# An encoder layer of Conformer convolution and dilated attention on one core: the order of a fused pair's sums, of its background, and of the q and k groups

## The chip, the cores and the metric

The kernel runs on one core of one Trainium2 chip. The metric is the device time of one launch in microseconds (us). The core's engines each work through a queue of their own: TensorE does the matmuls (PE; its loading of the stationary operand is shown as PEld), VectorE (DVE) and ScalarE (ACT) work on tiles, GpSimd (POOL) and SyncE (SP) issue transfers here.

## What is computed

One layer with 256 positions, width 4096, 16 heads of 128, and a convolution of 31 taps over 2048 channels, all float32:

```python
xn = rms_norm(x, norm_g[l])
h = jnp.einsum('bsd,de->bse', xn, w_in[l])          # 4096 x 14336
c_val, c_glu, c_gate, q, k, v, a_gate = jnp.split(h, split_pts, axis=-1)
conv_out = conformer_conv(c_val, c_glu, ...)        # GLU, depthwise conv31, LayerNorm, silu
conv_out = conv_out * jax.nn.silu(c_gate)
q, k = rms_norm(q, q_norm_g[l]), rms_norm(k, k_norm_g[l])   # per head
attn = longnet_mixture(q, k, v, rel_bias)           # three dilated windows, combined
attn_out = attn * jax.nn.silu(a_gate)
mixed = jnp.concatenate([conv_out, attn_out], axis=-1)
x = x + jnp.einsum('bse,ed->bsd', mixed, w_out[l])  # 4096 x 4096
```

## The kernel before

**Groups, pairs and parts.** The two large products are cut into 18 groups of 1024 columns: 14 of the input product (four conv, two gate, then qk and agv by turns, four of each: agv holds the attention's gate and v) and 4 of the output. A group runs through 16 pairs of 128-row blocks of the contraction; a pair's weights, 1 MB, are one transfer into one of three buffers `raw` (`load_pair`, L226, on SP's queue). In the text a pair's place in its group is its slot, counted from 0.

Float32 is done as sums of products of split numbers: a high part (`ScalarE` casts, `wh`) and a low part (`VectorE` subtracts, `wl`). A product of a split row block with a split weight takes three matmuls of 512 columns: high by high, low by high, high by low.

- A **plain pair** (`split_plain`, L973, and `Stream.plain`, L1139) takes 24 matmuls. ACT casts `wh` in two halves (L977), DVE subtracts 2048 columns for `wl` (L984).
- A **fused pair** (`split_fused`, L990, and `fused`, L1112) does a 2 x 2 block product with seven products instead of eight (Winograd's form of Strassen's scheme): 21 matmuls. It needs sums of the weight blocks (t1, t3, t4, t2) and sums of the row blocks (`block_sums`, s1 to s4). Its weights are made in four steps. Each casts on ACT and subtracts on DVE: `b` (b11 and b21, L1001 and L1002), b22 (L1014, L1015), t13 and t42 (L1001 and L1002 again). The sums themselves are taken in place in `raw` by DVE: the pair for t13 at L1016, those for t42 at L1023 and L1024. The four products m1, m5, m6 and m7 of all fused pairs of a group gather in four PSUM banks of their own and are combined by `add_more` (L1167).

Groups 0 and 1 work on x without its RMS factor and use `split_one` and `products`; while group 1 runs, `split_xn` makes the normalised rows `nh`, `nl` that all later input groups use. Groups 2 to 7 have fused pairs at slots 2, 4, 6, 8 and 10, groups 8 to 13 none. The first output group has three (slots 12 to 14), the others seven (slots 2, 4, 6, 7, 9, 10, 12).

**What sets the order.** Each engine's queue is written in program order, as the code runs: the code is a planner in Python. `Stream.step` issues the next step of weight splitting as soon as its buffers are free (four tiles `ws` of 2048 columns, and up to four `c4` tiles near fused pairs), and PE's matmuls free them. Between matmuls, `pump` gives turns to generators (the lanes): convolution, transposes through DRAM, head norms, softmax, and so on. This is the background. It goes by two budgets `left` for DVE and ACT, filled by `credit` with a share FILL of the time that PE takes, and spent by the costs that the generators yield; `now` is the planner's clock. `fused` calls `pump` twice within a fused pair.

The convolution's taps are done in two ways: on DVE alone (L524, four instructions a tap), or as products on ACT (L484, four instructions into the one tile `cp`) that DVE adds in one instruction (L515). The first way is used only in groups without fused pairs.

Heads need a PSUM bank from the tag `side`; fused pairs hold all of these, so the first fused pair of the first output group stands behind the last head (`busy`).

Of the kernel before, what the change touches and what calls it, by code (L numbers as in the profile page):

```python
# [17 lines left out]
P = 128  # L18
S = 256
# [16 lines left out]
FILL, SAVED = (0.96, 0.93), (700, 700)  # L36
# [3 lines left out]
C4 = 17  # L40
# [52 lines left out]
ONE, TWO = ((1, 0),), ((0, 2), (1, 0))  # L93
# [31 lines left out]
def layer_kernel(  # L125
# [35 lines left out]
    def rsqrt(src, shape, mul, eps, name):  # L161
# [8 lines left out]
        yield cost  # L170
        nc.scalar.activation(r, v, AF.Sqrt)
        yield
# [32 lines left out]

    def credit(ns):

        for i in range(2):
            left[i] += FILL[i] * ns
        now[0] += ns  # L210
# [19 lines left out]
    xh, xl, xsum = {}, {}, {}  # L230
# [40 lines left out]
    def split_xn(k):  # L271
# [10 lines left out]
        xh[k], xl[k] = h, l  # L282
        yield 415
        if k % 2 and k // 2 in FUSED[FUSED_IN[0]]:
            sums = block_sums(k // 2, src_of=xT, parts=(xh, xl), out=xsum, name="xs")
            if k < KT // 2:
                yield from sums
            else:
                late_sums.append(sums)

    split_gens, late_sums = [], deque()

    def run(gen):
        for cost in gen:
            spend(*(cost if isinstance(cost, tuple) else (cost or 0,)))

    def split_more():

        for gen in list(split_gens):
            cost = next(gen, None)  # L300
            if cost is None:
                split_gens.remove(gen)
            else:
                spend(*(cost if isinstance(cost, tuple) else (cost,)))

    def block_sums(j, src_of, parts, out, name):
# [14 lines left out]
        nc.scalar.copy(both[:, 0], t)  # L321
        nc.vector.tensor_sub(both[:, 1], t, both[:, 0].bitcast(F32))
# [7 lines left out]
        yield 690, 620  # L330
# [5 lines left out]
    def finish_rstd():  # L336
        tot = const.tile([P, 2], F32, name="sstot")
        nc.vector.reduce_sum(tot, ss, axis=AX.X)
        r = yield from rsqrt(tot, [P, 2], 1.0 / D, NORM_EPS, "rx")
# [127 lines left out]
    cp = const.tile([P, 4, S], F32, name="cp")  # L467


    taps, made = deque(), []  # L470
# [4 lines left out]
    def conv_products(cb):  # L475
# [4 lines left out]
        while taps and taps[-1][0] == cb:  # L480
            _, k = taps.pop()
            sh, lo, hi = conv_range(k)
            for t in range(4):
# [4 lines left out]
                if t == 3:  # L488
                    made.append((k, now[0] + 1500))
                if t % 2:  # L490
                    yield 0, 1020
            while made:
                yield

    def conv_gen(cb):
# [15 lines left out]
        while n_left:  # L511
            if made and made[0][1] <= now[0]:
                k, _ = made[0]
                _, lo, hi = conv_range(k)
                nc.vector.tensor_add(c[:, :, lo:hi], c[:, :, lo:hi], cp[:, :, lo:hi])  # L515
# [16 lines left out]
            if n_left == 6 and cb < 3 and cb + 1 not in fetched:  # L532
                fetched.add(cb + 1)
                post_lane.add(fetch_gen(cb + 1))
# [31 lines left out]
    def ln_gen():  # L566
# [5 lines left out]
        yield  # L572
# [3 lines left out]

        sq = [t4(f"sq{cb}") for cb in range(4)]
        for cb in range(4):
            nc.scalar.activation(sq[cb], cT[cb], AF.Square)
            yield 0, 1050  # L580
        pv = yield from channel_mean(sq, "va", sq[0])
        r = yield from rsqrt(pv[:, :S], [P, S], 1.0, LN_EPS, "rc")
        for cb in range(4):
            nc.vector.tensor_mul(cT[cb], cT[cb], bcast4(r))
            yield 1220
        for cb in range(4):
# [44 lines left out]
    def qk_norm(hg):  # L631
        st = sb.tile([P, 16], F32, tag="rs_small", bufs=6, name=f"ssqk{hg}")
        both = (qt[hg], kt[hg])
        for i, src in enumerate(both):
            v = src.rearrange("p a b -> p (a b)")
            for n in range(8):
# [5 lines left out]
                if n % 4 == 3:  # L642
                    yield 0, 1960
        r = yield from rsqrt(st, [P, 16], 1.0 / DH, NORM_EPS, f"rqk{hg}")
        for i, src in enumerate(both):
            v = src.rearrange("p a b -> p (a b)")
            for n in range(8):
# [4 lines left out]
                if n % 4 == 3:  # L652
                    yield 0, 1600
        yield from turn_far([qt[hg], kt[hg]], f"turn_qk{hg}")
# [4 lines left out]
    def head_gen(hg, hh):  # L659
# [32 lines left out]
        yield 1370  # L692
        for it in range(2):
# [4 lines left out]
        yield 0, 1380  # L698
        nc.vector.reciprocal(z, z)
        yield 160  # L700
        for it in range(2):
# [3 lines left out]
        yield 0, 1000  # L705
        tmp = t2(f"turn_p{h}")
# [54 lines left out]
    post_lane, head_lane, gate_lane, mix_lane = Lane(2), Lane(4), Lane(1, ()), Lane(1)  # L761
# [570 lines left out]
```

## Time and profile before

| what | us |
|---|---|
| three runs: lowest, median, highest | 1691.78, 1695.71, 1695.84 |
| the profiled execution | 1695.4 |
| its span, from the first to the last instruction | 1693.6 |
| mean granted TensorE clock | 0.990 |

A line of the timeline gives start, length, engine, source line, operation, the tile written and the tiles read (without their numbers), and in brackets how long the engine had been idle before and what it waited for. A line of the waits gives who waited for whom, with the time in all, how often, and the longest. A line of the busy time by stretch gives the stretch, its length, then for each engine its busy time and number of instructions, the granted clock, the share of the transfers and their GB/s. A line of the groups gives busy time and mean ns of one, then the engine's idle time just before them.

### The profile page before, as it was taken

How to read it: one execution, taken by the hardware profiler on the slowest of the kernel's cores; microseconds unless marked ns; L12 is line 12 of the kernel's file. 1: busy time of each engine (PE TensorE's matmuls, PEld its weight loads, DVE VectorE, ACT ScalarE, POOL GpSimd, SP SyncE). 2: the span in 40 equal slices, each digit the busy share in tenths (PEclk: the TensorE clock that was granted, in tenths of full speed). 3: DMA queues.
4: the chain of work that ended last, by engine and by line, in shares of the span. 5: the costliest groups of instructions: out<-in, count | busy, mean ns of one | idle time of the engine just before them, and what ended most of it. 6: DMA issues, size and time to landing. Idle time of an engine off the chain costs nothing.

```text
span 1693.6 us, 18693 instructions
## 1 busy us (share of the span) xinstructions
PE 1613.2 (95%) x6904; PEld 1296.9 (77%) x6904; DVE 1280.0 (76%) x1414; ACT 977.2 (58%) x1525; POOL 99.0 (6%) x184
## 2 busy tenths in 40 slices
PE   9999999999999989899999999999999999798988
PEld 7888768777777767678887887788888877586866
DVE  6669878787777777779788788877476677787877
ACT  6756545465646455577676657558667444444443
POOL 0000000000000000011110300102112100000000
PEclk9999999999999999999999999999999999999999
DMA  9766456454655554478675754866676745464653
GB/s 381 273 250 250 149 183 206 183 199 158 227 208 187 189 172 175 151 249 267 210 236 191 251 198 174 260 238 230 213 265 214 247 160 181 176 223 178 220 189 124
DMA packets 64523, 357.22 MB, mean 211 GB/s; under 512 B 9104, under 2 KB 11920, under 8 KB 27824
## 3 DMA queue, kind: packets, MB, share of 16 engines
q1 hardware_dynamic: 54096, 326.38, 54.4%
q0 software_dynamic: 10048, 29.37, 5.8%
q8 instruction: 54, 0.88, 0.2%
q10 hardware_dynamic: 288, 0.28, 0.1%
q14 instruction: 37, 0.30, 0.1%
HBM read 337.09 MB, written 18.91 MB: 210 GB/s over the span
## 4 chain that ended last, share of the span: by engine, by line
PE 52%; DVE 24%; ACT 14%; issue 9%; DMA 1%; ACTq 0%; DVEq 0%
PE c L1147 24%; PE c L1149 12%; ACT wh L977 7%; ACT t L1001 5%; DVE t L1002 5%; DVE b L1002 4%; PE acc L885 3%; PE acc L886 3%; PE acc L888 3%; DVE wl L984 3%; DVE raw L1016 3%; PE c L1162 2%; DVE raw L1024 2%; DVE raw L1023 2%; DVE b L1015 2%
## 5 line engine op out<-in xcount | busy, mean ns | idle before, releaser
L984 DVE TENSOR_TENSOR wl<-raw,wh 128x2048 fp32r<-128x2048 f32 x202 | 461.9, 2289 | 188.4 <-ACT wh L977 187.1
L977 ACT CAST wh<-raw 128x1024 fp32r<-128x1024 f32 x404 | 401.7, 1044 | 137.8 <-PE c L1149 95.6
L1147 PE MATMUL c<-wh,nh 128*128 128x512 f32 x1200 | 471.7, 393 | 4.0 <-ACT wh L977 3.8
L1149 PE MATMUL c<-wh,nl 128*128 128x512 f32 x1200 | 469.9, 392 | 0.0
L1001 ACT CAST t<-raw 128x1024 fp32r<-128x1024 f32 x108 | 113.2, 1048 | 336.0 <-DVE raw L1016 186.1
L1147 PE MATMUL c<-wl,nh 128*128 128x512 f32 x1200 | 299.6, 392 | 0.0
L1147 PEld LDWEIGHTS c<-wh,nh 128*128 128x128 f32 x1200 | 227.9, 190 | 54.9 <-ACT wh L977 6.5
L1149 PEld LDWEIGHTS c<-wh,nl 128*128 128x128 f32 x1200 | 227.3, 189 | 47.7
L1147 PEld LDWEIGHTS c<-wl,nh 128*128 128x128 f32 x1200 | 225.2, 188 | 47.0 <-DVE wl L984 0.3
L1002 DVE TENSOR_TENSOR t<-raw,t 128x1024 fp32r<-128x1024 f32 x108 | 132.3, 1225 | 126.0 <-ACT t L1001 126.0
L484 ACT ACTIVATE cp<-a,wT 128x241 f32<-128x241 f32 (+13 forms) x288 | 125.1, 491 | 108.7 <-DVE cT L515 108.6
L1147 PE MATMUL c<-wh,mh 128*128 128x512 f32 x288 | 113.9, 396 | 0.0
L1149 PE MATMUL c<-wh,ml 128*128 128x512 f32 x288 | 113.5, 394 | 0.0
L956 DVE TENSOR_TENSOR wh<-raw,wh 128x1024 fp32r<-128x1024 f32 x63 | 77.0, 1222 | 39.5 <-ACT wh L955 39.1
L885 PE MATMUL acc<-wh,xh 128*128 128x512 f32 x256 | 99.9, 390 | 0.5 <-ACT xh L264 0.5
L886 PE MATMUL acc<-wh,xl 128*128 128x512 f32 x256 | 99.7, 390 | 0.0
L955 ACT CAST wh<-raw 128x1024 fp32r<-128x1024 f32 x63 | 66.2, 1050 | 42.6 <-PE acc L888 26.9
L515 DVE TENSOR_TENSOR cT<-cT,cp 128x964 f32<-128x964 f32 (+13 forms) x72 | 84.6, 1175 | 2.9 <-ACT cp L484 0.8
L524 DVE SCALAR_TENSOR_TENSOR cT<-a,wT,cT 128x255 f32<-128x255 f32 (+8 forms) x192 | 80.9, 474 | 0.7
L1147 PE MATMUL c<-wl,mh 128*128 128x512 f32 x288 | 71.5, 390 | 0.0
L888 PE MATMUL acc<-wh,xh 128*128 128x512 f32 x256 | 69.1, 389 | 0.0
L1002 DVE TENSOR_TENSOR b<-raw,b 128x1024 fp32r<-128x1024 f32 x54 | 65.8, 1219 | 0.7 <-ACT b L1001 0.7
(321 smaller groups left out, 2129.9 us busy)
## 6 DMA issues: line engine op xcount, KB each, us to landing
raw<-in_w_dram SPq DMA_DIRECT2D x286, 1024.0 KB, 4.9
xT<-in_x_cols_dram SPq DMA_DIRECT2D x15, 512.0 KB, 6.8
x<-in_x_dram SPq DMA_DIRECT2D x8, 512.0 KB, 8.5
xr<-in_x_dram SPq DMA_DIRECT2D x8, 512.0 KB, 6.5
out_dram<-xr SPq DMA_DIRECT2D x15, 256.0 KB, 7.0
T<-bias_dram SPq DMA_DIRECT2D x16, 192.0 KB, 5.8
raw<-in_w_dram SPq DMA_DIRECT2D x3, 512.0 KB, 6.0
turn_qk0d<-turn_qk POOLq DMA_DIRECT2D x2, 512.0 KB, 8.6
```

The costliest lines, as they stand in the source:

```text
L484: nc.scalar.activation(cp[:, t, lo:hi], a[:, t, lo + sh : hi + sh], AF.Copy, scale=wT[:, 4 * cb + t, k : k + 1],)
L515: nc.vector.tensor_add(c[:, :, lo:hi], c[:, :, lo:hi], cp[:, :, lo:hi])
L524: nc.vector.scalar_tensor_tensor(c[:, t, lo:hi], a[:, t, lo + sh : hi + sh], wT[:, 4 * cb + t, k : k + 1], c[:, t, lo:hi], op0=ALU.mult, o ...
L885: nc.tensor.matmul(a, hs, wp, start=k == 0, stop=False)
L886: nc.tensor.matmul(a, ls, wp, start=False, stop=False)
L888: nc.tensor.matmul(a, hs, wp, start=False, stop=k == KT - 1)
L977: nc.scalar.copy(h[:, 1024 * k : 1024 * k + 1024], raw_tiles[u][:, k])
L984: nc.vector.tensor_sub(l, src, h.bitcast(F32))
L1001: nc.scalar.copy(h, src)
L1002: nc.vector.tensor_sub(l, src, h.bitcast(F32))
L1147: nc.tensor.matmul(acc, a[s][0], b[e], start=begin, stop=False)
L1149: nc.tensor.matmul(acc, a[s][1], b[e], start=False, stop=False)
```

## The change

- In `split_fused` the sum for t13 moves from the second step to the end of the first, and the sums for t42 from the third to the end of the second.
- `fused` no longer calls `pump`; while a fused pair or a row block is waited for, `more_rows` gives turns to the row splits alone. In groups with fused pairs the background's share of ACT's time (FILL) falls from 0.93 to 0.72.
- The order of groups 6 to 13 becomes qk, qk, agv, qk, agv, qk, agv, agv.
- Products of taps have two tiles `cp`, used by turns; a product is added, and its tile used again, 3 us of the planner's clock later. Taps on DVE alone may now also be issued in fused groups, with 0.4 us of budget to spare.
- Generators wait 3 us of the planner's clock (`settled`) between steps of one engine and the next engine's step on them.
- Group 1 is done by `Stream.group` with plain pairs; `split_xn` follows it pair by pair, at most four at a time, into `xnh`, `xnl`, and the sums of its rows are made right there.
- The first output group has four fused pairs (slots 8, 10, 12, 14) in another order of pairs. A plain pair's two casts are two steps. One `c4` buffer fewer (16).

```diff
-FILL, SAVED = (0.96, 0.93), (700, 700)
+FILL, SAVED = ((0.95, 0.72), (0.96, 0.93)), (700, 700)
+SETTLED = 3000
-C4 = 17
+C4 = 16
...
-for _hg in range(4):
-    GROUPS.append(("qk", _hg, C_Q + 512 * _hg, C_K + 512 * _hg))
-    GROUPS.append(("agv", _hg, C_AG + 512 * _hg, C_V + 512 * _hg))
+for _kind, _hg in zip("kkakakaa", (0, 1, 0, 2, 1, 3, 2, 3)):
...
-FUSED += [range(3)] + 3 * [range(7)]
+FUSED += [range(4)] + 3 * [range(7)]
-ORDERS += [(3, 4, 5, 8, 9, 10, 11, 12, 13, 14, 15, 6, 0, 1, 2, 7)]
+ORDERS += [(4, 5, 8, 9, 10, 11, 12, 13, 0, 14, 1, 15, 2, 6, 3, 7)]
...
+    def settled():
+        end = now[0] + SETTLED
+        while now[0] < end:
+            yield
...
-            left[i] += FILL[i] * ns
+            left[i] += FILL[state["taps"]][i] * ns
...
-            if made and made[0][1] <= now[0]:
-                k, _ = made[0]
+            if made and made[0][2] <= now[0]:
+                k, cp, _ = made.popleft()
                 nc.vector.tensor_add(c[:, :, lo:hi], c[:, :, lo:hi], cp[:, :, lo:hi])
-                made.clear()
+                cps.append((cp, now[0] + SETTLED))
...
-            elif taps and state["taps"]:
+            elif taps and left[0] > (0 if state["taps"] else 400):
...
+    def more_rows():
+        if split_gens:
+            split_more()
+        else:
+            pump(PRODUCT)
...
             def one():
-                both("b", blocks()[:, 0:2, :], ("b11", "b21"))
+                r = blocks()
+                both("b", r[:, 0:2, :], ("b11", "b21"))
+                nc.vector.tensor_add(r[:, 0:4:3, :], r[:, 0:3:2, :], twice(r[:, 3, :]))
+                spend(1225)
...
             def two():
                 nc.scalar.copy(h, r[:, 2, :])
                 nc.vector.tensor_sub(l, r[:, 2, :], h.bitcast(F32))
-                nc.vector.tensor_add(r[:, 0:4:3, :], r[:, 0:3:2, :], twice(r[:, 3, :]))
-                spend(1910, 620)
+                nc.vector.tensor_add(r[:, 2, :], r[:, 0, :], r[:, 2, :])
+                nc.vector.tensor_add(r[:, 1, :], r[:, 2, :], r[:, 1, :])
+                spend(2050, 620)
...
             def three():
                 both("t13", blocks()[:, 0:4:3, :], ("t1", "t3"))
-                r = blocks()
-                nc.vector.tensor_add(r[:, 2, :], r[:, 0, :], r[:, 2, :])
-                nc.vector.tensor_add(r[:, 1, :], r[:, 2, :], r[:, 1, :])
-                spend(1365)
...
-            return [(ONE, high), (ONE, low)]
+            return [(ONE, first), (NONE, lambda: high(1)), (ONE, low)]
...
+                if g == 1 and slot % 2 == 0 and slot < n_pairs - 2:
+                    load_xT(2 * slot + 4, 4, nc.sync)
...
                 if slot < n_pairs - 1:
                     self.plain(u, j, rows, one, slot == 0)
+                    if g == 1:
+                        split_gens.extend(split_xn(k) for k in (2 * j, 2 * j + 1))
...
-                if i in (2, 5):
-                    pump()
...
-        if g >= FUSED_IN[0]:
+        if g > 0:
             stream.group(g)
```

How the instructions move is shown at three places. In the names the first number is that of the pair, 16 to a group; `wl` is the low part of a plain pair, `b`, `b22`, `t13` and `t42` are the four splits of a fused pair, and a row that writes `raw` is a sum taken in place.

First, VectorE in group 16, the third output group, slots 3 and 4 (pairs 259 and 260). Before:

```order
L984 TENSOR_TENSOR wl259_10909<-raw259_10791,wh259_10894 128x2048
L1002 TENSOR_TENSOR b_2601_10920<-raw260_10834,b_2600_10919 128x1024
L1015 TENSOR_TENSOR b22_260_10923<-raw260_10834,b22_260_10923 128x512
L1016 TENSOR_TENSOR raw260_10834<-raw260_10834 128x2x512
L1002 TENSOR_TENSOR t13_260_10936<-raw260_10834,t13_260_10936 128x1024
L1023 TENSOR_TENSOR raw260_10834<-raw260_10834 128x512
L1024 TENSOR_TENSOR raw260_10834<-raw260_10834 128x512
L1002 TENSOR_TENSOR t42_260_10947<-raw260_10834,t42_260_10947 128x1024
```

And now:

```order
L1028 TENSOR_TENSOR wl259_10878<-raw259_10760,wh259_10863 128x2048
L1046 TENSOR_TENSOR b_2601_10889<-raw260_10803,b_2600_10888 128x1024
L1054 TENSOR_TENSOR raw260_10803<-raw260_10803 128x2x512
L1062 TENSOR_TENSOR b22_260_10893<-raw260_10803,b22_260_10893 128x512
L1063 TENSOR_TENSOR raw260_10803<-raw260_10803 128x512
L1064 TENSOR_TENSOR raw260_10803<-raw260_10803 128x512
L1046 TENSOR_TENSOR t13_260_10907<-raw260_10803,t13_260_10907 128x1024
L1046 TENSOR_TENSOR t42_260_10916<-raw260_10803,t42_260_10916 128x1024
```

The first sum moved from behind b22 to behind b, and the two small sums from behind t13 to ahead of it; t13 and t42 now follow each other.

Second, VectorE in group 2 (the first with fused pairs), the fused pair at slot 2 (pair 34), where `xs` and `xsp` are the sums of the rows for pair 8. Before:

```order
L1016 TENSOR_TENSOR raw34_1513<-raw34_1513 128x2x512
L1002 TENSOR_TENSOR t13_34_1652<-raw34_1513,t13_34_1652 128x1024
L1023 TENSOR_TENSOR raw34_1513<-raw34_1513 128x512
L1024 TENSOR_TENSOR raw34_1513<-raw34_1513 128x512
L314 TENSOR_TENSOR xs_8_1665<-xT16_1143 128x128
L315 TENSOR_TENSOR xs_8_1665<-xs_8_1665,xT16_1143 128x128
L317 TENSOR_TENSOR xs_8_1665<-xT16_1143 128x128
L318 TENSOR_TENSOR xs_8_1665<-xT16_1143,xs_8_1665 128x128
L322 TENSOR_TENSOR xsp8_1670<-xs_8_1665,xsp8_1670 128x512
L1002 TENSOR_TENSOR t42_34_1673<-raw34_1513,t42_34_1673 128x1024
```

And now:

```order
L1046 TENSOR_TENSOR b_341_1589<-raw34_1490,b_340_1588 128x1024
L1054 TENSOR_TENSOR raw34_1490<-raw34_1490 128x2x512
L1062 TENSOR_TENSOR b22_34_1593<-raw34_1490,b22_34_1593 128x512
L1063 TENSOR_TENSOR raw34_1490<-raw34_1490 128x512
L1064 TENSOR_TENSOR raw34_1490<-raw34_1490 128x512
L1046 TENSOR_TENSOR t13_34_1614<-raw34_1490,t13_34_1614 128x1024
L1046 TENSOR_TENSOR t42_34_1625<-raw34_1490,t42_34_1625 128x1024
```

The five instructions of the row sums have left the fused pair (they stand in group 1 now).

Third, ScalarE in group 4, the fused pair at slot 4 (pair 68), where `cp` is a product of a tap. Before:

```order
L1001 CAST b_680_2908<-raw68_2820 128x1024
L1014 CAST b22_68_2912<-raw68_2820 128x512
L1001 CAST t13_68_2925<-raw68_2820 128x1024
L484 ACTIVATE cp_77<-a0_1047,wT_73 128x247 x2
L1001 CAST t42_68_2938<-raw68_2820 128x1024
L484 ACTIVATE cp_77<-a0_1047,wT_73 128x247 x2
L977 CAST wh69_2961<-raw69_2862 128x1024 x2
```

And now:

```order
L1045 CAST b_680_2880<-raw68_2795 128x1024
L1061 CAST b22_68_2885<-raw68_2795 128x512
L1045 CAST t13_68_2899<-raw68_2795 128x1024
L1045 CAST t42_68_2908<-raw68_2795 128x1024
L495 ACTIVATE cp1_78<-a0_1065,wT_73 128x244 x2
L1022 CAST wh69_2931<-raw69_2837 128x1024 x2
```

No product stands between the casts of t13 and t42 any more; one pair of products is left, ahead of the next plain pair's wh.

More of the change, by code (lines that the diff above doesn't have):

```diff
@@ L170, in rsqrt @@
         yield cost
+        if wait:
+            yield from settled()
         nc.scalar.activation(r, v, AF.Sqrt)
-        yield
+        yield 0, 1400 + n
+        if wait:
+            yield from settled()
         nc.vector.reciprocal(r, r)
@@ L281, in split_xn @@
         nc.vector.tensor_sub(l, src, h.bitcast(F32))
-        xh[k], xl[k] = h, l
+        xnh[k], xnl[k] = h, l
         yield 415
         if k % 2 and k // 2 in FUSED[FUSED_IN[0]]:
[L285 to L295, printed above, removed]
+            yield from block_sums(k // 2, src_of=xT, parts=(xnh, xnl), out=xsum, name="xs")
+    split_gens = deque()
     def split_more():
-        for gen in list(split_gens):
+        for gen in list(split_gens)[:4]:
             cost = next(gen, None)
@@ L329, in block_sums @@
         out[j] = names
-        yield 690, 620
+        yield 690
     def by_block(ap):
@@ L465, in fetch_gen @@
         yield 0, 1150
-    cp = const.tile([P, 4, S], F32, name="cp")
-    taps, made = deque(), []
+    taps, made = deque(), deque()
+    cps = deque((const.tile([P, 4, S], F32, name=f"cp{i}"), 0) for i in range(2))
     def conv_range(k):
@@ L571, in ln_gen @@
         nc.scalar.copy(mu, pm[:, :S])
-        yield
+        yield 0, 400
+        yield from settled()
         for cb in range(4):
@@ L585, in ln_gen @@
             yield 1220
+        yield from settled()
         for cb in range(4):
@@ L692, in head_gen @@
         yield 1370
+        yield from settled()
         for it in range(2):
@@ L705, in head_gen @@
         yield 0, 1000
+        yield from settled()
         tmp = t2(f"turn_p{h}")
@@ L827, in evacuate_sum @@
         fused = (g, e) in more_tiles
-        if not fused and s == 0:
+        if not fused and s == 0 and (g, e) != (1, 1):
             plain_tiles[(g, e)] = half_tile(g, e)
-        tile_, pair = (more_tiles if fused else plain_tiles)[(g, e)]
+        tile_, pair = (more_tiles if fused else plain_tiles).get((g, e)) or plain_tiles[(g, 0)]
         t = pair[:, s, :]
```

109 lines of the change are left out of this document (67 added, 42 removed).

## The prediction

> **What bounds the kernel now.** I read the page first, then the busy time by stretch, then the waits, then the engines' timelines in one fused pair. The page's engine line is tempting: TensorE (PE) busy 95%, so little to win.
>
> ```profile
> span 1693.6 us, 18693 instructions
> PE 1613.2 (95%) x6904; PEld 1296.9 (77%) x6904; DVE 1280.0 (76%) x1414; ACT 977.2 (58%) x1525; POOL 99.0 (6%) x184
> ```
>
> But a matmul is drawn 0.39 us long and the next one starts before it ends, so busy time hides lost time. The pace is better read from starts. In the timeline of PE in a stretch without waits, one plain pair begins at 773.85 and the next at 779.29:
>
> ```profile
> 768.57 3.61 PE L678 MATMUL psc<-qk,near_q 128*128 128x256 f32 x16
> 771.83 2.18 PE L1147 MATMUL c<-wl,nh 128*128 128x512 f32 x8
> 773.85 0.39 PE L1147 MATMUL c<-wh,nh 128*128 128x512 f32 x1
> ...
> 779.29 0.39 PE L1147 MATMUL c<-wh,nh 128*128 128x512 f32 x1
> ```
>
> So 24 matmuls take 5.44 us, 0.2267 us each; a fused pair (21) takes 4.76 at that pace. The 16 records of four heads take 771.83 - 768.57 = 3.26 us, 0.204 each. Now the busy time by stretch, cut where groups begin (start; groups 0-1; 2-7; 8-13; output; columns are length, busy of PE, PEld, DVE, ACT and POOL with counts, PE clock, DMA):
>
> ```profile
> 0.00:5.60 5.60, 4.10 (x22) 3.91 (x22) 0.59 (x2) 2.00 (x4) 0.20 (x4) 1.00 0.61 180
> 5.60:180.40 174.80, 174.75 (x769) 144.17 (x770) 126.25 (x193) 113.33 (x184) 2.87 (x5) 1.00 0.77 286
> 180.40:747.30 566.90, 528.79 (x2217) 417.62 (x2216) 435.19 (x409) 313.25 (x459) 11.50 (x21) 0.98 0.53 188
> 747.30:1301.90 554.60, 549.17 (x2420) 453.27 (x2419) 427.09 (x518) 377.57 (x683) 74.06 (x135) 1.00 0.68 225
> 1301.90:1689.90 388.00, 356.41 (x1482) 277.90 (x1480) 290.12 (x294) 171.01 (x199) 10.39 (x19) 0.98 0.54 192
> ```
>
> Groups 2-7 need 6 x (11 x 24 + 5 x 21) = 2214 matmuls, 501.9 us: 65.0 are lost. Groups 8-13 need 2304 and some 116 records of heads and means, 522.3 + 23.7 = 546.0: 8.6 lost. Output needs 375 + 3 x 363 = 1464 and 16 records, 335.2: 52.8 lost. Groups 0-1 lose 0.7. So 127 us are lost, nearly all in the two stretches that hold fused pairs, whose clock is also 0.98 where the others show 1.00. The floor is 1693.6 - 127.1 = 1566.5. The waits name the place:
>
> ```profile
> DVE t L1002 <- ACT t L1001: 126.0, 108, 1.5
> ACT wh L977 <- PE c L1149: 95.6, 44, 6.9
> PE m L1036 <- ACT t L1001: 41.6, 44, 2.7
> PE m L1038 <- DVE t L1002: 27.6, 55, 0.5
> ```
>
> PE waits for the split of the sums (t, that is t13 and t42 of a fused pair), and in 108 splits of 108 VectorE (DVE) stands idle for ScalarE (ACT) first. One plain and one fused pair of group 16, DVE and then ACT:
>
> ```profile
> 1510.45 2.29 DVE L984 TENSOR_TENSOR wl<-raw,wh 128x2048 fp32r<-128x2048 f32 x1 [0.67 <-ACT wh L977]
> 1512.66 1.22 DVE L1002 TENSOR_TENSOR b<-raw,b 128x1024 fp32r<-128x1024 f32 x1
> 1513.79 0.69 DVE L1015 TENSOR_TENSOR b<-raw,b 128x512 fp32r<-128x512 f32 x1
> 1514.39 1.22 DVE L1016 TENSOR_TENSOR raw<-raw 128x1024 f32<-128x1024 f32 x1
> 1516.81 1.23 DVE L1002 TENSOR_TENSOR t<-raw,t 128x1024 fp32r<-128x1024 f32 x1 [1.20 <-ACT t L1001]
> 1517.95 0.69 DVE L1023 TENSOR_TENSOR raw<-raw 128x512 f32<-128x512 f32 x1
> 1518.67 0.69 DVE L1024 TENSOR_TENSOR raw<-raw 128x512 f32<-128x512 f32 x1
> 1520.56 1.23 DVE L1002 TENSOR_TENSOR t<-raw,t 128x1024 fp32r<-128x1024 f32 x1 [1.19 <-ACT t L1001]
> 1522.45 2.29 DVE L984 TENSOR_TENSOR wl<-raw,wh 128x2048 fp32r<-128x2048 f32 x1 [0.67 <-ACT wh L977]
> ```
> ```profile
> 1510.32 1.05 ACT L1001 CAST b<-raw 128x1024 fp32r<-128x1024 f32 x1
> 1511.27 0.61 ACT L1014 CAST b<-raw 128x512 fp32r<-128x512 f32 x1
> 1515.72 1.05 ACT L1001 CAST t<-raw 128x1024 fp32r<-128x1024 f32 x1 [3.84 <-DVE raw L1016]
> 1519.47 1.05 ACT L1001 CAST t<-raw 128x1024 fp32r<-128x1024 f32 x1 [2.70 <-DVE raw L1024]
> 1520.43 1.99 ACT L977 CAST wh<-raw 128x1024 fp32r<-128x1024 f32 x2
> ```
>
> The unit repeats every 12.0 us (1510.45 to 1522.45), where PE needs 45 x 0.2267 = 10.2. The two engines take turns: DVE sums, ACT casts the sum, DVE takes the difference, twice over.
>
> **The sums, moved.** Nothing is added; the order shows raw (the sum for t13) right behind b, and both later sums ahead of t13's difference. Working the after unit from the starts above: wl to b 2.21, b to raw 1.13, raw to b22 1.14 (as t13 to the next sum), b22 to the first small sum 0.60, to the second 0.72, from there to ACT's cast of t42 0.80, to wh 0.96, to the next wl 2.02: 9.58 us. The cast of t13 (1.33 behind its sum's start, 1.05 long) now lies beside b22 and the small sums; DVE's wait before t42 shrinks to about 0.1. What is late next is PE: 9.58 is under 10.2. Each unit had lost 1.8 and more, and now gains 0.6 of lead. Two fused pairs in a row (two places in groups 15-17) remain DVE's: 1.13 + 1.14 + 0.60 + 0.72 + 0.72 + 1.14 + 1.14 = 6.59 against 4.76, so 1.8 of lead is spent at each. The lead on entry comes from t42 of the first fused pair; in group 3, before, the pair's first matmul and the end of t42 are:
>
> ```profile
> 287.81 0.39 PE L1036 MATMUL m<-b,nh 128*128 128x512 f32 x1
> ...
> 289.64 1.22 DVE L1002 TENSOR_TENSOR t<-raw,t 128x1024 fp32r<-128x1024 f32 x1 [1.17 <-ACT t L1001]
> ```
>
> PE needs t42 18 matmuls after 287.81, at 291.9; it is done at 290.86, 1.0 early. With the sums moved it comes 2.4 sooner (12.0 - 9.58), 3.4 early.
>
> **Background out of fused pairs.** In group 2 the five sums of xn leave the fused pair; elsewhere a conv product or a transpose stood there, as here, ahead of a plain pair's wl:
>
> ```profile
> 571.55 1.89 DVE L417 STREAM_TRANSPOSE turn_g<-gate 128x512 f32<-128x512 f32 x3
> ```
>
> What was in the fused stretch must go into plain slots, where DVE was busy 427.09 of 554.6 us, so it is covered. What stays in the stretch (one or two conv adds a group) costs 1.2 us each at most, against the lead above. On ACT a pair of products (2 x 0.49) now stands between t42 and wh: such a unit is 9.58 + 0.98 = 10.56 by ACT, 0.36 over PE; four of them spend 1.4 of 3.4 us. If that cover fails, the next part's rival A gives the price.
>
> **Two tiles of products.** These rows price a tap:
>
> ```profile
> L484 ACT ACTIVATE cp<-a,wT 128x241 f32<-128x241 f32 (+13 forms) x288 | 125.1, 491 | 108.7 <-DVE cT L515 108.6
> L515 DVE TENSOR_TENSOR cT<-cT,cp 128x964 f32<-128x964 f32 (+13 forms) x72 | 84.6, 1175 | 2.9 <-ACT cp L484 0.8
> L524 DVE SCALAR_TENSOR_TENSOR cT<-a,wT,cT 128x255 f32<-128x255 f32 (+8 forms) x192 | 80.9, 474 | 0.7
> ```
>
> In the changed order 49 taps instead of 72 go through ACT. DVE gains 23 x (4 x 0.474 - 1.175) = 16.6 us of work, ACT loses 23 x 4 x 0.491 = 45; the second tile takes ACT's 108.6 us of waiting for DVE out of its queue. Both lie in plain slots, off PE's path: nothing, or up to 5 us if DVE falls behind there.
>
> **q and k sooner, the waits called settled, group 1 in pairs, four fused pairs in the first output group.** Settled only issues later, to work that has slack; PE still carries the same head matmuls. The last heads' po come in the fifth pair of the first output group instead of the sixth, ahead of its first fused pair (now ninth, then thirteenth); no wait is expected, 0 to 5. Group 1 lost nothing and does the same matmuls; its seven more loads of xT pass through SP's queue ahead of weights: 0 to 5. One more fused pair saves 3 matmuls, 0.7.
>
> **The clock.** A wait is followed by slow matmuls:
>
> ```profile
> 302.00:304.00 2.00, 0.90 (x3) 0.47 (x4) 1.23 (x1) 2.00 (x4) 0.00 (x0) 1.00 0.00 0
> 304.00:306.00 2.00, 2.00 (x6) 1.59 (x7) 0.78 (x1) 2.00 (x3) 0.00 (x0) 0.59 0.51 119
> 306.00:308.00 2.00, 2.00 (x6) 1.55 (x6) 2.00 (x2) 0.66 (x2) 0.00 (x0) 0.56 0.96 406
> ```
>
> By the two rows at 0.98, 0.02 x (566.9 + 388.0) = 19 of the 127 us are this. I take it to go with the waits, but 3. [...]
>
> **The sum.** Floor 1566.5 - 0.7 = 1565.8; groups 8-13 keep 8.6 (3 if the 5.4 us go in which PE was idle there, 554.60 - 549.17); groups 2-7 keep 1 each, 6 (0 to 24); output keeps 8 (2 in the first, 3 in the second, which enters behind a late fused pair, 1.5 in each other; 0 to 20); clock 3 (0 to 8). Span 1591.4. The profiled execution took 1695.4 for its span of 1693.6, 1.8 more, and stands 0.3 under the median of 1695.71: 1593.
>
> **Rivals.** A, the cover is thin: the cast chain moves from DVE's wait to ACT's queue. Units with a product and its add take 10.56 + 0.5, 0.86 over, 24 times: 21; entries find no lead, 10 groups x 1.5: 15; double fused pairs cost 1.8 x 6: 11; slots lost to clock, half of before: 10. With 8.6: 1565.8 + 8.6 + 57 = 1631, and 1633 with the 1.8. For it: 95.6 us in which wh already waited for PE's buffers, so lead cannot grow freely. Against: 3.4 us of lead on entry.
>
> B, the clock loss is not due to the waits: 1593 - 3 + 19 = 1609. Against: the two stretches at 0.98 are the two with the waits. [...]
>
> C, slower: buffers. If the cast of wh has to wait until PE has finished the fused pair before it, PE stands through both casts, 2.02 us, in each unit: 10.2 + 2.02 + 0.1 = 12.3 against 12.0, in 40 units 12 us more, 1707. It decides from 1.8 us of such wait a unit on. For it: the row of 95.6 us, 44 times, 2.2 each. Against: before, these waits lay mostly in plain stretches, and the tile's former user, the wh before it, is read out 3.6 us into a plain pair.
>
> D, the casts stay bound by something else and the unit stays 12.0: 1695. The order shows the sums moved, so little is left for it.
>
> **Chances and range.** Forecast 0.68, A 0.20, B 0.05, C 0.03, D 0.04. The likeliest gives 1593. Its own bounds are 1571 (all of it hidden: 1565.8 + 3 + 1.8) and 1628 (24, 20 and 8 with the 8.6); I take 1572, and to take in A I end at 1640. About 0.3% (5 us) is what a measurement can tell: faster by more 0.93, within 0.04, slower 0.03.
>
> **What would show it.** Right: DVE's wait for t under 30 us instead of 126; units of about 10.2 us in fused stretches; PE waits for t under 20 us in all; clock 1.00 there; groups 8-13 unchanged near 555 us. Rival A: units of 10.5 to 11 with wh or cp ending the wait. C: wh waiting for PE inside fused stretches. Wrong altogether: a span above 1640, or losses outside the fused stretches.

## The result and the profile after

| | us |
|---|---|
| changed kernel, four runs: lowest, median, highest | 1574.82, 1575.35, 1577.37 |
| kernel before, four runs beside them: lowest, median, highest | 1691.78, 1695.55, 1695.84 |
| profiled execution of the changed kernel, and its span | 1575.05, 1573.3 |

The ratio of the changed kernel to the one before is 0.9298, 95% interval 0.9282 to 0.9314: 120 us less. The forecast was 1593 in a range of 1572 to 1640, so the time lies inside, 18 under the likeliest value.

The page's engine line of the changed kernel, then its waits of PE:

```profile
span 1573.3 us, 18570 instructions
PE 1565.2 (99%) x6901; PEld 1294.9 (82%) x6901; DVE 1298.7 (83%) x1473; ACT 928.4 (59%) x1421; POOL 99.2 (6%) x184
```
```profile
PE po L740 <- DMA pr<-turn_p15d: 1.7, 1, 1.7
PE m L1082 <- DVE t L1046: 1.3, 1, 1.3
```

The two rows that carried the loss before (41.6 and 27.6 us for t) have become one wait of 1.3 us. The busy time by stretch, cut where groups begin (groups 0-1, 2-7, 8-13, output; columns as before):

```profile
5.48:181.44 175.96, 175.69 (x770) 143.86 (x769) 122.87 (x176) 107.96 (x172) 2.87 (x5) 1.00 0.77 284
181.44:683.28 501.84, 501.84 (x2216) 415.54 (x2214) 455.92 (x471) 288.83 (x395) 8.26 (x15) 1.00 0.60 212
683.28:1230.89 547.61, 547.61 (x2421) 454.45 (x2420) 421.68 (x524) 357.31 (x656) 78.05 (x142) 1.00 0.69 229
1230.89:1569.50 338.61, 335.62 (x1478) 276.77 (x1476) 296.86 (x300) 172.31 (x196) 9.79 (x18) 1.00 0.61 219
```

The clock is 1.00 in each, and in groups 2 to 13 PE is never idle in these records. Against the count of matmuls: groups 2-7 take 501.84 us where the count gives 501.9 (65.0 more before); groups 8-13 take 547.61 where it gives 546.0 (8.6 more before); the output takes 338.6 where it gives 335.2 - 0.7 = 334.5 (52.8 more before).

A plain and a fused pair of group 16 on DVE, then ACT from the same unit:

```profile
1416.35 2.29 DVE L1028 TENSOR_TENSOR wl<-raw,wh 128x2048 fp32r<-128x2048 f32 x1 [0.67 <-ACT wh L1022]
1418.55 1.22 DVE L1046 TENSOR_TENSOR b<-raw,b 128x1024 fp32r<-128x1024 f32 x1
1419.81 1.23 DVE L1054 TENSOR_TENSOR raw<-raw 128x1024 f32<-128x1024 f32 x1
1420.95 0.69 DVE L1062 TENSOR_TENSOR b<-raw,b 128x512 fp32r<-128x512 f32 x1
1421.67 0.69 DVE L1063 TENSOR_TENSOR raw<-raw 128x512 f32<-128x512 f32 x1
1422.40 0.69 DVE L1064 TENSOR_TENSOR raw<-raw 128x512 f32<-128x512 f32 x1
1423.01 2.50 DVE L1046 TENSOR_TENSOR t<-raw,t 128x1024 fp32r<-128x1024 f32 x2
1426.29 2.29 DVE L1028 TENSOR_TENSOR wl<-raw,wh 128x2048 fp32r<-128x2048 f32 x1 [0.77 <-ACT wh L1022]
```
```profile
1421.15 1.06 ACT L1045 CAST t<-raw 128x1024 fp32r<-128x1024 f32 x1 [3.37 <-DVE raw L1054]
1423.20 1.06 ACT L1045 CAST t<-raw 128x1024 fp32r<-128x1024 f32 x1 [0.99 <-DVE raw L1064]
1424.26 2.00 ACT L1022 CAST wh<-raw 128x1024 fp32r<-128x1024 f32 x2
```

ACT now casts t13 (1421.15) while DVE is at b22 and the small sums, so DVE goes from one t to the other without a break (one row, x2, 2.50 us). The unit repeats after 9.94 us instead of 12.0, under the 10.2 that PE needs. Over the whole kernel the group of these splits, 110 of them, has 2.8 us of idle time in front, against 126 before:

```profile
L1046 DVE TENSOR_TENSOR t<-raw,t 128x1024 fp32r<-128x1024 f32 x110 | 134.2, 1221 | 2.8
```

### The profile page after: what moved, and what is told of

The parts are those of the page before. It is cut to its first block, busy times and chain, and to the rows that moved or that the text cites. A ratio compares the mean times of both kernels' runs of the same rounds, so it can differ in the third digit from the quotient of the medians.

```text
span 1573.3 us, 18570 instructions
## 1 busy us (share of the span) xinstructions
PE 1565.2 (99%) x6901; PEld 1294.9 (82%) x6901; DVE 1298.7 (83%) x1473; ACT 928.4 (59%) x1421; POOL 99.2 (6%) x184
## 4 chain that ended last, share of the span: by engine, by line
PE 87%; issue 6%; DMA 4%; DVE 1%; ACT 1%; POOL 0%; SPq 0%; DVEq 0%; POOLq 0%; ACTq 0%
PE c L1195 40%; PE c L1197 20%; PE c L1210 3%; PE m L1082 3%; PE m L1080 3%; PE m L1081 3%; PE c L1080 2%; PE c L1081 2%; PE c L1082 2%; PE acc L927 2%; PE acc L924 2%; PE acc L925 2%; PE c L1212 2%; DMA raw<-in_w_dram 1%; PE psc L696 1%
## 5 line engine op out<-in xcount | busy, mean ns | idle before, releaser
L1028 DVE TENSOR_TENSOR wl<-raw,wh 128x2048 fp32r<-128x2048 f32 x217 | 496.4, 2289 | 174.3 <-ACT wh L1022 165.6
L1022 ACT CAST wh<-raw 128x1024 fp32r<-128x1024 f32 x434 | 433.6, 1048 | 255.4 <-PE c L1197 185.1
L533 DVE SCALAR_TENSOR_TENSOR cT<-a,wT,cT 128x252 f32<-128x252 f32 (+10 forms) x284 | 117.7, 472 | 0.5
L495 ACT ACTIVATE cp<-a,wT 128x241 f32<-128x241 f32 (+7 forms) x196 | 84.5, 488 | 9.9 <-DVE cT L524 9.8
L1054 DVE TENSOR_TENSOR raw<-raw 128x1024 f32<-128x1024 f32 x55 | 67.4, 1225 | 1.9
L1195 PEld LDWEIGHTS c<-wh,mh 128*128 128x128 f32 x280 | 52.6, 188 | 10.9
L1197 PEld LDWEIGHTS c<-wh,ml 128*128 128x128 f32 x280 | 52.6, 188 | 10.9
L1195 PEld LDWEIGHTS c<-wl,mh 128*128 128x128 f32 x280 | 52.6, 188 | 10.9
L998 DVE TENSOR_TENSOR wh<-raw,wh 128x1024 fp32r<-128x1024 f32 x31 | 37.9, 1224 | 24.8 <-ACT wh L997 24.8
L524 DVE TENSOR_TENSOR cT<-cT,cp 128x964 f32<-128x964 f32 (+7 forms) x49 | 57.1, 1166 | 1.1
```

Source lines behind the costliest of these rows:

```text
L495: nc.scalar.activation(cp[:, t, lo:hi], a[:, t, lo + sh : hi + sh], AF.Copy, scale=wT[:, 4 * cb + t, k : k + 1],)
L533: nc.vector.scalar_tensor_tensor(c[:, t, lo:hi], a[:, t, lo + sh : hi + sh], wT[:, 4 * cb + t, k : k + 1], c[:, t, lo:hi], op0=ALU.mult, o ...
L1022: nc.scalar.copy(h, raw_tiles[u][:, k])
L1028: nc.vector.tensor_sub(l, src, h.bitcast(F32))
L1054: nc.vector.tensor_add(r[:, 0:4:3, :], r[:, 0:3:2, :], twice(r[:, 3, :]))
L1195: nc.tensor.matmul(acc, a[s][0], b[e], start=begin, stop=False)
```

## The experiments

Times are medians. "Over the change" means against 1575.35 us of the changed kernel.

**The sums alone.** The kernel before with only the sums moved:

```diff
             def one():
-                both("b", blocks()[:, 0:2, :], ("b11", "b21"))
+                r = blocks()
+                both("b", r[:, 0:2, :], ("b11", "b21"))
+                nc.vector.tensor_add(r[:, 0:4:3, :], r[:, 0:3:2, :], twice(r[:, 3, :]))
...
             def two():
...
-                nc.vector.tensor_add(r[:, 0:4:3, :], r[:, 0:3:2, :], twice(r[:, 3, :]))
...
+                nc.vector.tensor_add(r[:, 2, :], r[:, 0, :], r[:, 2, :])
+                nc.vector.tensor_add(r[:, 1, :], r[:, 2, :], r[:, 1, :])
...
             def three():
                 both("t13", blocks()[:, 0:4:3, :], ("t1", "t3"))
-                r = blocks()
-                nc.vector.tensor_add(r[:, 2, :], r[:, 0, :], r[:, 2, :])
-                nc.vector.tensor_add(r[:, 1, :], r[:, 2, :], r[:, 1, :])
...
```

> The kernel before with the sums of a fused pair moved and nothing else. Theory S (the order of the sums is the gain: a unit of a plain and a fused pair falls from 12.0 us to 9.6, under TensorE's 10.2): 1595 to 1620 us, with VectorE's wait for t gone (under 30 us from 126). Rival P (what stood between the steps of a fused pair, the background, is the gain): 1665 to 1690. Rival O (neither alone: the new order of groups and group 1 in pairs carry it): 1650 to 1690.

Measured: 1590.13 us, ratio to before 0.9381 (0.9354 to 0.9408): 104 of the 120 us. Its longest waits of PE, and its busy time in groups 2-7 and in groups 8-13 (cut where its own groups begin):

```profile
PE c L1147 <- ACT wh L977: 3.8, 3, 1.3
PE m L1038 <- DVE t L1002: 3.7, 6, 1.2
PE m L1036 <- ACT t L1001: 2.4, 2, 1.3
```
```profile
180.34:690.16 509.82, 505.43 (x2215) 416.11 (x2214) 437.68 (x409) 314.42 (x459) 11.54 (x21) 1.00 0.58 209
690.16:1244.73 554.57, 549.34 (x2422) 453.81 (x2420) 427.51 (x518) 377.69 (x683) 74.23 (x135) 1.00 0.67 225
```

The waits for t fall from 69 to 6 us. What is left is 4.4 us of PE idle in groups 2-7 (509.82 - 505.43), all but 0.37 of it in the first 31 us of group 2, and 5.2 in groups 8-13, close to the 5.4 that the kernel before showed there. Against the changed kernel groups 2-7 take 8.0 us more (509.82 - 501.84) and groups 8-13 take 7.0 more (554.57 - 547.61). So the sums explain the fused stretches but for the head of group 2, and something else in the change took away the rest.

**The sums put back.** The changed kernel with its sums in their old places:

```diff
             def one():
...
-                nc.vector.tensor_add(r[:, 0:4:3, :], r[:, 0:3:2, :], twice(r[:, 3, :]))
...
             def two():
...
+                nc.vector.tensor_add(r[:, 0:4:3, :], r[:, 0:3:2, :], twice(r[:, 3, :]))
...
-                nc.vector.tensor_add(r[:, 2, :], r[:, 0, :], r[:, 2, :])
-                nc.vector.tensor_add(r[:, 1, :], r[:, 2, :], r[:, 1, :])
...
             def three():
                 both("t13", blocks()[:, 0:4:3, :], ("t1", "t3"))
+                r = blocks()
+                nc.vector.tensor_add(r[:, 2, :], r[:, 0, :], r[:, 2, :])
+                nc.vector.tensor_add(r[:, 1, :], r[:, 2, :], r[:, 1, :])
...
```

> The changed kernel with the sums put back to their old places. Theory S: a unit is 12.0 us again whatever else is changed, 1.8 over TensorE in 16 units of the output and 24 of groups 2 to 7 less some lead: 1650 to 1685 us, and the TensorE clock falls again to about 0.98 in these stretches. Rival P: 1575 to 1610. Rival O: 1575 to 1600.

Measured: 1677.71 us, ratio 0.9898 (0.9869 to 0.9926), 102 over the change. The waits of PE are those of the kernel before again:

```profile
PE m L1080 <- ACT t L1045: 36.5, 39, 1.3
PE m L1082 <- DVE t L1046: 22.7, 44, 0.5
```

Taken away or put in alone, the sums are worth 102 to 104 us; all the rest together is worth 15 to 17.

**Background back in fused pairs.** The changed kernel with its turns inside `fused` and the old share of ACT:

```diff
-FILL, SAVED = ((0.95, 0.72), (0.96, 0.93)), (700, 700)
+FILL, SAVED = ((0.96, 0.93), (0.96, 0.93)), (700, 700)
...
                     self.free((u, freed))
+                if i in (2, 5):
+                    pump()
```

> The changed kernel with the two turns of background inside a fused pair back, and ScalarE's share at 0.96 and 0.93 in all groups. Theory S: the unit has 0.6 us to spare and some 3 us of lead, so a little is lost in groups 2 to 7 alone: 1575 to 1595 us. Rival P: 1640 to 1690. Rival O: 1575 to 1580.

Measured: 1575.59 us, 0.2 over the change, ratio 0.9295 (0.9268 to 0.9322).

**Background out, alone.** The kernel before without the two turns:

```diff
-                if i in (2, 5):
-                    pump()
```

> The kernel before without the two turns of background inside a fused pair, and nothing else. Theory S: the unit stays 12.0 us in the output groups (no gain there) and at 12.0 to 12.5 in groups 2 to 7: 1670 to 1695 us. Rival P: 1590 to 1630. Rival O: 1685 to 1700.

Measured: 1696.71 us against 1694.4 beside it, ratio 1.0013 (1.0002 to 1.0024). Where the sums stand early, the background in fused pairs is covered; where they stand late, taking it out wins nothing, probably because DVE was waiting for ACT in any case (126.0 us for t in the kernel before). This part of the change is worth nothing in either kernel.

**One tile of products.** The changed kernel with one `cp`:

```diff
-    cps = deque((const.tile([P, 4, S], F32, name=f"cp{i}"), 0) for i in range(2))
+    cps = deque((const.tile([P, 4, S], F32, name=f"cp{i}"), 0) for i in range(1))
```

> The changed kernel with one tile for the products of taps instead of two. Theory T (in groups 8 to 13 TensorE waited because ScalarE's next product stood at the head of its queue for the one tile, with the cast of wh behind it): three to five waits of 1.3 to 1.5 us come back, 1579 to 1583 us. Rival N (the planner's settled waits took these waits away): 1574 to 1577.

Measured: 1573.51 us, ratio 0.9291 (0.9275 to 0.9308), not to be told from the change. In the profiled execution, the slowest of its four runs, PE waits for wh twice:

```profile
PE c L1195 <- ACT wh L1022: 3.3, 2, 2.8
```

One wait, 0.5 us, lies in groups 8 to 13. The long one, 2.8 us, lies before them, between 100 and 680 us (PE is busy 577.13 of these 580.00 us); what held its cast up is not shown. So one tile alone does not bring the waits of groups 8 to 13 back. But it does not bring the old way back either: with one tile that rests 3 us only 33 taps go through ACT (49 in the change, 72 before), and ACT waits 13.3 us for their adds, not 108.6.

**No settling.** The changed kernel where `settled` returns at once:

```diff
-        end = now[0] + SETTLED
-        while now[0] < end:
-            yield
+        return
+        yield
```

> The changed kernel whose generators no longer wait 3 us of the planner's clock between engines (the two tiles of products keep theirs). Theory T: 1574 to 1577 us. Rival N: waits of ScalarE and VectorE for each other at the head of their queues come back in groups 8 to 13, 1579 to 1586.

Measured: 1575.31 us, ratio 0.9291 (0.9276 to 0.9307). No difference either, and no wait of PE in groups 8 to 13. The products' own rests of 3 us are not in `settled` and stayed.

**More work per fused pair.** How much cover is left? One and two reductions more for DVE, behind the first sum of each of the 55 fused pairs; nobody reads their result:

```diff
+    idle = const.tile([P, 2], F32, name="idle")
...
                 nc.vector.tensor_add(r[:, 0:4:3, :], r[:, 0:3:2, :], twice(r[:, 3, :]))
+                for _ in range(1):
+                    nc.vector.reduce_max(idle, r[:, 1:3, :], axis=AX.X)
```

> The changed kernel with one more VectorE instruction of about 1.2 us in each fused pair, right behind the first sum (it reduces two blocks of raw to a tile that nobody reads). Theory S with its numbers (unit 9.58 us of VectorE and ScalarE against TensorE's 10.20, some 3.4 us of lead on entry to a fused stretch): the unit is 10.8, the lead covers groups 2 to 7, and the output groups with two fused pairs in a row lose about 5 us each: 1588 to 1605 us. Rival Q (VectorE has far more room than 0.6 us a unit, since steps overlap more than the starts say): 1574 to 1580.

> The same with two such instructions. Theory S: the unit is 12.0 us, as in the kernel before: groups 2 to 7 lose about 6 us each, the output groups 6 to 14 each, and the TensorE clock falls: 1650 to 1685 us. Rival Q: 1580 to 1620.

Measured: 1621.30 us with one, ratio 0.9566 (0.9547 to 0.9585), and 1691.88 with two, ratio 0.9984 (0.9973 to 0.9994). Both lie above what was expected. The waits of PE with one, and the row of the added work, then the waits with two:

```profile
PE m L1085 <- DVE t L1047: 28.7, 30, 1.6
```
```profile
L1057 DVE TENSOR_REDUCE idle<-raw 128x2 f32<-128x1024 f32 x55 | 66.6, 1211 | 0.0
```
```profile
PE m L1085 <- DVE t L1047: 61.5, 44, 1.6
PE c L1085 <- DVE b L1065: 20.1, 19, 2.2
```

The first 66.6 us of added work cost some 46, so 21 us of it were hidden; the second cost 70.6, all of it and 4 more. With one, the span is 47.4 us over the changed kernel's; of PE's 28.7 us of waits for t, 16.7 lie in groups 2-7 and 12.0 in the output. The expectation had nothing in groups 2-7: it had counted with units of 9.58 us and forgotten that many there also hold a pair of products on ACT (10.6 us, below), which have no slack to give but the lead. For the output it had about 5 us in each group with fused pairs in a row; the unit there is 9.94 and not 9.58, and fused pairs in a row cost more than was worked out (below). These reasons are argued from the rows and not tested by themselves.

**The sums of the rows back in group 2.** The changed kernel, where the sums for the row blocks of pairs 8 and 10 stand in the fused pairs of group 2 again:

```diff
-            yield from block_sums(k // 2, src_of=xT, parts=(xnh, xnl), out=xsum, name="xs")
+            sums = block_sums(k // 2, src_of=xT, parts=(xnh, xnl), out=xsum, name="xs")
+            if k < KT // 2:
+                yield from sums
+            else:
+                late_sums.append(sums)
...
+                if g == 2 and late_sums and slot % 2:
+                    run(late_sums.popleft())
```

> The kernel after, with the sums of the row blocks of pairs 8 and 10 put back into group 2's fused pairs, between t13 and t42. Theory R (these sums are the largest part of the 15 us that moving the weights' sums alone leaves over the kernel after): PE waits again for t between 190 and 215 us, 2 to 5 waits of 0.5 to 1.3 us, the clock falls there, and the time is 1578 to 1582 us. Rival (group 2 is short in the kernel after because its background is gone, wherever the row sums stand): no wait over 0.5 us there and 1574 to 1577 us.

Measured: 1578.26 us, ratio 0.9314 (0.9301 to 0.9326), 2.7 over the next experiment on the same chip (1577.08 to 1579.98 against 1575.18 to 1575.69, four runs each). DVE between t13 and t42 of the second of these pairs, then what PE waited for there:

```profile
204.99 1.22 DVE L1054 TENSOR_TENSOR t<-raw,t 128x1024 fp32r<-128x1024 f32 x1
206.12 0.28 DVE L328 TENSOR_TENSOR xs<-xT 128x128 f32<-128x128 f32 x1
...
207.82 0.69 DVE L337 TENSOR_TENSOR xsp<-xs,xsp 128x512 fp32r<-128x512 f32 x1 [0.69 <-ACT xsp L335]
208.77 1.23 DVE L1054 TENSOR_TENSOR t<-raw,t 128x1024 fp32r<-128x1024 f32 x1 [0.26 <-ACT t L1053]
```
```profile
208.79 0.50 PE L1088 MATMUL m<-t,xsp 128*128 128x512 f32 x1 [1.03 <-ACT t L1053]
210.05 0.50 PE L1090 MATMUL m<-t,xsp 128*128 128x512 f32 x1 [0.53 <-DVE t L1054]
```

Without them t42 would start at 206.12; it starts 2.65 later, and PE, not yet far behind the weights at the head of the first fused group, waits. Half of that theory holds: PE waits there again, three times, but the clock stays at 1.00 in this execution, and 2.7 us is not the largest part of 15.

**One tile, used again soon.** Does the rest of the tile keep ACT from standing in front of a product that DVE has not added yet? The changed kernel with one tile and a rest of 0.5 us instead of 3:

```diff
-    cps = deque((const.tile([P, 4, S], F32, name=f"cp{i}"), 0) for i in range(2))
+    cps = deque((const.tile([P, 4, S], F32, name=f"cp{i}"), 0) for i in range(1))
...
-                cps.append((cp, now[0] + SETTLED))
+                cps.append((cp, now[0] + 500))
```

> The kernel after, with one tile for products that may be written again 0.5 us of the planner's clock after the add that reads it, instead of two that rest 3 us. Theory H (the rest keeps ACT from standing at the head of its queue until DVE has added, and thereby the casts behind it in time): ACT waits for DVE's cT 60 to 110 us in all instead of 9.8, PE waits 3 to 8 times by about 1.2 us for wh or wl in groups 8 to 13, and the time is 1579 to 1585 us. Rival (the casts are issued so far ahead that such a wait is covered): at most one such wait, and 1574 to 1577 us.

Measured: 1575.56 us, ratio 0.9297 (0.9284 to 0.9309). ACT's wait for the add, here and in the kernel with the sums alone:

```profile
ACT cp L495 <- DVE cT L524: 12.7, 8, 4.5
```
```profile
ACT cp L484 <- DVE cT L515: 105.2, 42, 7.7
```

It stays short, so the tile's rest of 3 us is not by itself what took ACT's 105 us of waiting away. But here too only 35 taps go through ACT, and two things of the old way were not put back: a product was added after 1.5 us of the planner's clock instead of 3, and the products' turn asked for 0.8 us of ACT's budget instead of 1.5 (an edit that the list of the change does not name).

**The old first output group.** The changed kernel with three fused pairs in a row there:

```diff
-FUSED += [range(4)] + 3 * [range(7)]
+FUSED += [range(3)] + 3 * [range(7)]
...
-ORDERS += [(4, 5, 8, 9, 10, 11, 12, 13, 0, 14, 1, 15, 2, 6, 3, 7)]
+ORDERS += [(3, 4, 5, 8, 9, 10, 11, 12, 13, 14, 15, 6, 0, 1, 2, 7)]
```

> The kernel after, with the first output group as it was: three fused pairs, in one run at slots 12 to 14, instead of four with a plain pair between each two. One fused pair fewer is 3 matmuls more, 0.7 us. Theory F (a run of three fused pairs costs DVE 6.59 us each against 4.76 us of matmuls, 3.7 us more for two of them, of which a lead of some 3 us covers most): 0.7 to 3 us more, 1576 to 1578.5 us. Rival (a run outruns the cover whatever the lead, and the clock falls behind it): PE waits for t of 2 us and more in all in that group, and 1579 to 1584 us.

Measured: 1577.53 us, ratio 0.9308 (0.9295 to 0.9321), 2.0 over the experiment before it. PE's waits for t are 1.8 us in all (1.3 in the changed kernel), so the first theory holds: 0.7 us of the 2.0 are the three matmuls more.

**A sixth fused pair.** If PE's own work is all that is left, fewer matmuls should pay. The changed kernel with one fused pair more in each of groups 2 to 7:

```diff
-FUSED = [(2, 4, 6, 8, 10) if g in FUSED_IN else () for g in range(N_IN)]
+FUSED = [(2, 4, 6, 8, 10, 12) if g in FUSED_IN else () for g in range(N_IN)]
```

> The kernel after, with a sixth fused pair (slot 12) in each of groups 2 to 7: 18 matmuls of 0.2267 us fewer, 4.1 us. Theory (PE's own work is all that is left, DVE and ACT keep up with fused and plain pairs in turn): 1570.5 to 1572.5 us. Rival (the products of taps and the transposes that lose their room come back as waits in groups 8 to 13, or DVE falls behind in units that hold products, 10.6 us against 10.2): 1575 to 1590 us.

Measured: 1594.57 us, ratio 0.9409 (0.9397 to 0.9422): 19 slower than the change, with 18 matmuls fewer. PE's longest wait, and POOL's first DMA for the softmax of head 13; then POOL's in the changed kernel:

```profile
PE po L740 <- DMA pr<-turn_p13d: 13.9, 1, 13.9
```
```profile
1285.93 0.56 POOL L391 DMA_DIRECT2D turn_p13d<-turn_p  x1 [34.11 <-DVE turn_p L729]
```
```profile
1224.18 0.57 POOL L391 DMA_DIRECT2D turn_p13d<-turn_p  x1 [5.36 <-DVE turn_p L729]
```

DVE nearly keeps up with the fused pairs (3.6 us of waits). But the background has lost its plain slots, the last heads come 62 us later, and they are needed ahead of the first fused pair of the output. PE stands for them, 13.9 us in one piece, and the clock falls to 0.50 (third from the end):

```profile
1290.00:1300.00 10.00, 5.61 (x13) 3.63 (x13) 2.96 (x9) 1.02 (x2) 6.52 (x12) 0.50 0.25 79
```

The rival was right in its mechanism, work that loses its room comes back as a wait, and wrong in the place, the output and not groups 8 to 13; its range ended at 1590. No experiment gave a version that beats the changed kernel by more than the runs can tell.

## Why the prediction was right, and where its sum was off

**The mechanism held.** The unit of the output was worked to 9.58 us and is 9.94: the large sum starts 1.26 behind b (worked 1.13), the first small sum 0.72 behind b22 (0.60), wh 1.06 behind the cast of t42 (0.96). It stayed under 10.2, so nothing hung on it. A unit with a pair of products was worked to 10.56; in group 3 it is 287.65 - 277.05 = 10.60:

```profile
275.97 1.16 DVE L524 TENSOR_TENSOR cT<-cT,cp 128x964 f32<-128x964 f32 x1
277.05 2.29 DVE L1028 TENSOR_TENSOR wl<-raw,wh 128x2048 fp32r<-128x2048 f32 x1
...
287.65 2.29 DVE L1028 TENSOR_TENSOR wl<-raw,wh 128x2048 fp32r<-128x2048 f32 x1 [1.45 <-ACT wh L1022]
```

The lead was put at 3.4 us on entry. At this place t42's low part is done at about 276.1, just as the add in the first row begins, and PE first reads it at 279.81, in the sixth of its seven products:

```profile
279.81 0.39 PE L1082 MATMUL m<-t,xsp 128*128 128x512 f32 x1
```

That is 3.7 us, and it carries the units that run 0.4 over PE's pace. (The prediction counted 18 matmuls up to this reading; the sixth product takes t2, a part of t42, so it is 17, or 0.2 us less.) The added reductions fit it from the other side: 21 us were hidden, some 2 for each of the ten groups with fused pairs.

**The sum was off by 18 us, in four terms, all set too high.** Groups 2-7 were to keep 6 us and keep none. The output was to keep 8 and keeps 4.1, of which two waits on PE are 3.0 (po 1.7, t 1.3). The clock was to cost 3 and costs nothing at 1.00. Groups 8-13 were to keep 8.6 and keep 1.6: there the prediction's words "groups 8-13 unchanged near 555 us" were wrong, they took 547.61. Against this, groups 0-1 lost 1.2 more than before (175.96 - (174.80 - 0.7) = 1.9, from 0.7), which the prediction had at 0 to 5. Together 6 + 3.9 + 3 + 7.0 - 1.2 = 18.7 of the 18.1 in the span (1591.4 - 1573.3). The prediction's cuts at 747.30 and 1301.90 are not quite where these groups of the kernel before begin (746.98 and 1302.02): its groups 8-13 lost 9.0 us and not 8.6, which changes nothing here.

The failed step is the one that gave "nothing" to the taps, the order of q and k, and the settled waits outside the fused stretches. The row of 5.4 us of PE idle in groups 8-13 stood there, and the bound with "3 if the 5.4 us go" was the right one. The sums alone leave those 5 us in place, and the whole change removes them. What they hang on can be read in the kernel with the sums alone. One of its four waits of PE in groups 8-13, then ACT just before:

```profile
858.00 0.50 PE L1147 MATMUL c<-wh,nh 128*128 128x512 f32 x1 [1.25 <-ACT wh L977]
```
```profile
856.13 0.89 ACT L484 ACTIVATE cp<-a,wT 128x244 f32<-128x244 f32 x2 [3.62 <-DVE cT L515]
856.92 1.98 ACT L977 CAST wh<-raw 128x1024 fp32r<-128x1024 f32 x2
```

ACT stood 3.62 us at a pair of products until DVE had added the tap before out of the one tile, and the cast that PE needed stood right behind it in ACT's queue. At the last of these waits the pair had stood 3.63 us, and at the same four places of the kernel before 1.47, 3.63, 3.24 and 3.63 us (behind the third of them PE waited for the wl made from that cast). So the prediction's reading that ACT's 108.6 us of waiting lie off PE's path was wrong for these four. Theory T, noted for the run with one tile, had named the right wait.

Which of the edits takes it away is not settled: the second tile, the settling, the tile's long rest and the background kept out were each undone in the changed kernel, and none brought more than 1.6 us of waiting back there, of the 5 (1.5 with the tile reused soon, for a sum of the LayerNorm and not for a cast). But in none of these did ACT wait for the adds as it did before. The old order of groups 6 to 13 and group 1 without pairs were not tried by themselves, nor the old taps beside the new order. Two causes may do the same work, so that undoing one shows nothing.

Of the 14.8 us that the sums alone leave over the change, 8.0 lie in groups 2-7, 7.0 in groups 8-13 and 0.7 in the output, and 1.1 less in groups 0-1. The row sums of group 2 bring back 2.7 of the 8.0; which edit is worth the rest of the 8.0 is not known. The 2.0 of the old first output group does not show as such in the kernel with the sums alone.

**The rivals.** A (a thin cover) fell: two fused pairs in a row take 7.05 us (b at 1428.49 and 1435.54 in group 16) instead of the 6.59 worked out, so each spends 2.3 us of lead, and yet PE's one wait for t is 1.3. B fell: the clock is 1.00 where the waits are gone, and 0.989 again with the sums put back. C fell: the wait of wh for PE grew from 95.6 to 185.1 us without a single wait of PE for wh in groups 2 to 13; a cast that waits for PE's buffers is a sign of lead here, not of loss. D fell with the unit's 9.94. The row for C, in the changed kernel:

```profile
ACT wh L1022 <- PE c L1197: 185.1, 85, 6.9
```

## What to carry to other kernels

When two engines hand a tile back and forth, look for the row where each waits for the other, and move the producer's step ahead of work that does not need it; here three sums a fused pair, moved, were worth 104 us, and all the other edits 15. Ask of a wait whether it is the slow engine's: ACT's waits for PE's buffers nearly doubled (95.6 to 185.1 us) while the kernel became 120 us faster. With the bound moved to PE, the room left to the background was the next thing to run out here: 18 matmuls fewer made the kernel 19 us slower, with one wait of 13.9 us for a head.

## What was not expected of the hardware

The clock fell to 0.50 after waits of at most 1.33 us in one kernel, and stayed at 1.00 in another with nearly the same waits just before. With the sums alone PE waited 1.04 and 0.53 us at 208 to 211, in the kernel with the row sums put back 1.03 and 0.53 at 208 to 210 (the last rows shown of it above). The kernel with the sums alone had also waited three times at 194 to 199, 2.45 us in all, where the other had waited once, 0.53; its clock was 1.00 in between. The waits at 208 to 211 with the sums alone:

```profile
209.32 0.50 PE L1036 MATMUL m<-t,xsp 128*128 128x512 f32 x1 [1.04 <-ACT t L1001]
210.58 0.50 PE L1038 MATMUL m<-t,xsp 128*128 128x512 f32 x1 [0.53 <-DVE t L1002]
```

The busy time of both in steps of 2 us (the PE clock is third from the end), first with the sums alone:

```profile
210.00:212.00 2.00, 1.47 (x6) 1.13 (x6) 1.33 (x2) 2.00 (x3) 0.00 (x0) 0.82 0.28 33
212.00:214.00 2.00, 2.00 (x6) 1.53 (x5) 2.00 (x2) 0.63 (x2) 0.00 (x0) 0.50 0.83 340
214.00:216.00 2.00, 2.00 (x9) 1.66 (x8) 1.97 (x3) 0.01 (x1) 0.00 (x0) 0.82 0.86 324
```

Then the row sums put back:

```profile
210.00:212.00 2.00, 1.95 (x9) 1.61 (x9) 1.33 (x1) 2.00 (x3) 0.00 (x0) 1.00 0.40 98
212.00:214.00 2.00, 2.00 (x10) 1.69 (x9) 2.00 (x2) 0.10 (x1) 0.00 (x0) 1.00 0.98 401
```

The loss in the first is (0.18 + 0.50 + 0.18) x 2 = 1.7 us: from 211.45 to 214.44 its matmuls start 0.43 us apart instead of 0.2267. In the second there is none; they start 0.23 apart from 210.38 on. So the length of a wait did not decide alone here. What else decided, these runs do not show.
